# A depthwise convolution as small Toeplitz matrices over permuted tokens, in a hybrid attention and convolution layer

## The chip, the cores and the metric

The kernel runs on all 8 cores of one Trainium2 chip, one sequence of the batch on each core, without communication. The metric is the device time of the slowest core, in microseconds (us). A second, slower state exists: in some executions the cores of one die show a lower TensorE clock (instead of 0.99) and the time is longer.

## The reference, cut to what matters

One decoder layer on x of 2048 tokens by 1024 features for each core:

```python
h = rmsnorm(x, g_mix_norm)
proj = h @ w_in + b_in                       # q | k | v | glu_in (2 x 512) | gates (2 x 1024)
y_attn = sliding_window_attention(q, k, v, sinks) @ w_attn_proj     # window 128, 8 heads of 64
a, b = split(glu_in);  z = a * sigmoid(b)    # GLU, 512 channels
z = causal_depthwise_conv(z, conv_w) + conv_b                       # 31 taps, one filter per channel
y_conv = silu(layernorm(z, ln_g, ln_b)) @ w_conv_proj + b_conv_proj
x = x + (gate0 * y_attn + gate1 * y_conv) @ w_out
x = x + (silu(gate) * up) @ w_ffn_down       # gate, up = rmsnorm(x) @ w_ffn_in, 2816 wide
return rmsnorm(x, g_final)
```

## The kernel before

Features lie on the partitions, tokens along the free dimension. Four parts follow one another: the **start** (first norms and projections), a **loop** over 16 attention blocks with the GLU and half of the convolution woven in, the **merge** (gates, the two output projections and the other half of the convolution), and the feed-forward part.

The convolution, 16 units (4 token groups by 4 channel tiles). SBUF-to-SBUF transfers lay four shifted copies of z under one another, so that a 128x32 weight block holds 4 taps of 32 channels on its diagonals. Four such blocks stand side by side in the array:

```python
def conv_unit(tg, c):
    for m in range(8):                       # 8 shifts x 4 taps = 32 taps
        for cg in range(4):                  # 4 x 32 channels, side by side
            mm(ps[bank][32*cg:32*(cg+1), :], wS[:, 4*c+cg, m, :],
               zs[half][:, c % 2, cg, 4*m:4*m+512], m == 0, m == 7, ..., tile_position=(0, 32*cg))
    act(y, ps[bank], AF.Identity, scale=0.5, bias=conv_b[...])     # ScalarE evicts ...
    act(ysq[tg][c], ps[bank], AF.Square, ...)                      # ... and squares, both from PSUM
    op("pool", tensor_copy(out=ybf[tg][c], in_=y))
# fill_zs(tg, half): 16 SBUF-to-SBUF transfers of 67.5 KB from zT
```

The start, in the order in which it is issued:

```python
for j, g in enumerate((0, 0, 0, 2, 4, 4)):
    load_qkv(j, r=["x.0.%d" % g])            # r: what the load waits for
load_x(1, xi[:, 1], r=["wqkv2"])             # second token group
...
p1_qk(0, (0, 1, 2)); p1_qk(0, (3, 4)); p1_v(0)      # projections of group 0
load_glu(0, r=["wqkv5"])                     # GLU weights, after x1
scores(0)
run(sqs)                                     # squares of x1; stats() below sums them on PE
glu_b(0, 0); glu_a(0, 0)
stats(); scores(1); run(norms[:4]); pv(0)
```

The softmax here doesn't subtract the row's maximum and nothing guards it: scores larger than these inputs give would overflow.

Of the kernel before, what the change touches and what calls it, by code (L numbers as in the profile page):

```python
# [14 lines left out]
D = 1024  # L15
T = 2048
# [181 lines left out]
def build_program():  # L198
# [10 lines left out]
    w_glu_d = din("w_glu", [4, 128, 2, 8, 128])  # L209
# [4 lines left out]
    NV = 210  # L214
    vec_d = din("vecs", [128, NV])
    wdiag_d = din("wdiag", [128, 16, 8, 32])
# [7 lines left out]
    def region(nbytes):  # L224
# [6 lines left out]
    X_OFF = region(66560)  # L231
# [3 lines left out]
    R_OFF = region(20480)  # L235
    VEC_OFF = region(NV * 4)
    HB_OFF = region(30 * 4)
    HLN_OFF = region(8 * 4)
# [8 lines left out]
    conv_b = vec[:, 30:34]  # L247
    ln_g = vec[:, 34:38]
    ln_b = vec[:, 38:42]
    bcp = vec[:, 42:50]  # L250
    g_mix = vec[:, 50:58]
    g_ffn = vec[:, 58:66]
    g_fin = vec[:, 66:74]
    sinks = vec[:, 74:82]
    bv_bc = vec[:, 82:210]
    hb = A.f32(HB_OFF, 30)
    hln = A.f32(HLN_OFF, 8)
# [5 lines left out]
    XB = X_OFF + 1024  # L263
# [5 lines left out]
    convT = A.bf16(CT_OFF, 4 * T).rearrange("p (c t) -> p c t", c=4)  # L269
    WS_OFF = R_OFF + 12288  # L270
    wS = A.bf16(WS_OFF, 16 * 8 * 32).rearrange("p (g m c) -> p g m c", g=16, m=8)
    ZSW = 544
    zs = [A.bf16(X_OFF + 8704 * i, 2 * 4 * ZSW).rearrange("p (h g t) -> p h g t", h=2, g=4)
          for i in range(2)]
    ysqoff = [[XB + 16384 + 1024 * c for c in range(4)]] * 4
    ysq = [[A.bf16(o, 512) for o in row] for row in ysqoff]

    hT = A.bf16(H_OFF, 8 * T).rearrange("p (c t) -> p c t", c=8)
    qT = A.bf16(M_OFF, 4 * T).rearrange("p (c t) -> p c t", c=4)
    kT = A.bf16(M_OFF + 16384, T)  # L280
    v_aug = A.bf16(M_OFF + 20480, 16 * 2 * 65).rearrange("p (n g d) -> p n g d", n=16, g=2)
    ZPAD = 32
    zT = A.bf16(M_OFF + 24640, 4 * (T + ZPAD)).rearrange("p (c t) -> p c t", c=4)
# [3 lines left out]
    NMIX = 4  # L287
    MIX_OFF = [R_OFF, R_OFF + 6144, W_OFF, W_OFF + 6144]
    w_mix_sb = [A.bf16(o, 3072).rearrange("p (s k m) -> p s k m", s=3, k=8) for o in MIX_OFF]
# [10 lines left out]
    class Tmp:  # L300
# [3 lines left out]
        def take(self, nbytes):  # L304
# [14 lines left out]
    yoff = [[CT_OFF + 4096 * c + 2048 for c in range(4)], [Y_OFF + 2048 * c for c in range(4)],  # L319
            [M_OFF + 16384 + 2048 * c for c in range(4)], [Y_OFF + 2048 * c for c in range(4)]]  # L320
    y32 = [[A.f32(o, 512) for o in row] for row in yoff]
    YB_OFF = t2.take(4 * 1024)
    ybfoff = [[CT_OFF + 4096 * c + 1024 for c in range(4)]] + [[YB_OFF + 1024 * c for c in range(4)]] * 3
    ybf = [[A.bf16(o, 512) for o in row] for row in ybfoff]
    ST_OFF = t2.take(2 * 2048)
    stA = A.f32(ST_OFF, 512)
    stB = A.f32(ST_OFF + 2048, 512)
    TB_OFF = t2.take(4096)
    tbl = A.f32(TB_OFF, 1024).rearrange("p (b t) -> p b t", b=2)
# [4 lines left out]
    iota_i = A.i32(PT_OFF, 128)  # L334

# [21 lines left out]
    NB2 = norm_bufs(PT_OFF, PT_OFF + 12288, PT_OFF + 8192, 4)  # L357
    w_out_sb = A.bf16(Y_OFF, 8 * 1024).rearrange("p (k n) -> p k n", k=8)
    nb = NB1

    ebuf = [A.f32(PT_OFF + 8192 * b, 2048).rearrange("p (k t) -> p k t", k=4) for b in range(2)]
# [64 lines left out]
    def load_x(tg, dst, r=()):  # L426
        for c in range(4):
            dma("sp", dst[:, 2 * c:2 * c + 2, :], x_d[tg, c], r=r,
                w=["x.%d.%d" % (tg, k) for k in (2 * c, 2 * c + 1)])
# [3 lines left out]
    M.claim("iota", PT_OFF, 512)  # L433
    claim_norm(NB1)
    for j in range(6):
        M.claim("wqkv%d" % j, R_OFF + 2048 * j, 2048)
    for c in range(4):
        M.claim("wglu%d" % c, W_OFF + 4096 * c, 4096)
# [4 lines left out]
    def load_glu(c, r=()):  # L443
        dma("pool", w_glu_sb[:, c], w_glu_d[c], r=r, w=["wglu%d" % c])
# [10 lines left out]
    op("pool", lambda e: e.memset(zT[:, :, 0:ZPAD], 0.0), w=["z_pad"])  # L455
    for j, g in enumerate((0, 0, 0, 2, 4, 4)):
        load_qkv(j, r=["x.0.%d" % g])
    load_x(1, xi[:, 1], r=["wqkv2"])
# [6 lines left out]
    M.claim("z_pad", M_OFF + 24640, 16640)  # L465
# [4 lines left out]
    def warm1():  # L470
        mm(ps[6][:, 0:256], ones[:, 0, :], ones.rearrange("p w m -> p (w m)"), True, True,
           r=["ones0", "ones1"], w=[P(6)])

# [4 lines left out]
    def sq_mm(stat, tg, src, c, first, last, eng="act"):  # L478
# [9 lines left out]
        def pe():  # L488
            for h in range(2):
                mm(ps[stat][:, :], ones[:, 0, :], n.sq[:, b, h, :], first and h == 0, last and h == 1,  # L490
                   r=["ones0", "sq%d" % b], w=[P(stat)])
# [34 lines left out]
    rot = Rot(list(range(7)))  # L526
    st_rot = Rot([7])
# [17 lines left out]
    def p1_tasks(tg):  # L545
        src = xi[:, tg % 2]
        stat = st_rot()
        pes = []

        def stats():  # L550
            for f in pes:
                f()
                if tg == 0:
                    warm(6)
            if tg == 0:
                warm(10)
            rstd(stat, tg)
# [6 lines left out]
    def qk_evac(tg, j, bank):  # L564
        dst, dn = (qT[:, j, tsl(tg)], "qT.%d" % tg) if j < 4 else (kT[:, tsl(tg)], "kT.%d" % tg)
        act(dst, ps[bank][:, :], AF.Identity, r=[P(bank), "vec"], w=[dn], bias=b_fm[:, j:j + 1])
# [10 lines left out]
    def p1_v(tg):  # L577
        bank = rot()
        for j in range(4):
            tt = 4 * tg + j  # L580
            for k in range(8):
                mm(ps[bank][:, j * 128:(j + 1) * 128], hT[:, k, tt * 128:(tt + 1) * 128],
                   w_qkv_sb[:, 5, k, :], k == 0, k == 7,
                   r=["wqkv5", "hT.%d.%d" % (tg, k)], w=[P(bank)])
# [671 lines left out]
```

## Time and profile before

| | before |
|---|---|
| median of 15 runs over all rounds | 902.55 us (the ten fast ones: 900.19 to 903.55, median 901.09) |
| spans of the 8 cores in the profiled run | 895.7 to 900.3 us, median 898.4 |
| TensorE busy | 868.3 us, 96% |
| convolution matmuls | 30.9 us |
| TensorE idle from 100 us to the end of the merge | about 1.5 us |

The main lines are shown in the prediction. Four more are needed later. First a window of the loop (length; then busy time and count of PE, PE's weight loads, VectorE, ScalarE and POOL; granted clock, DMA share, GB/s), then VectorE's timeline (start, length, what), the kind of transfer that fed the convolution (count, KB each, median us from issue to landing), and the longest piece of the chain that ended last.

```profile
100.00:150.00 50.00, 48.85 (x451) 24.60 (x453) 23.70 (x57) 30.83 (x51) 16.93 (x17) 1.00 0.39 83
...
27.79 3.30 DVE L397 TENSOR_TENSOR arena<-arena 128x1024 bf16<-128x1024 f32 x2
...
arena<-arena SPq DMA_DIRECT2D x128, 67.5 KB, 2.1
...
437.46 388.02 PE ps L391 x1797
```

In the loop PE is idle for about 1 us in 50. At 27.8 us VectorE squares its half of x1 (ScalarE squares the other half), early and undisturbed. The convolution's input comes in many small transfers that land in a median of 2.1 us. From 437 us on PE runs for 388 us in one piece: what is not won before that point is not won at all.

### The profile page before, as it was taken

The numbers are of one execution on the slowest core, as the hardware profiler recorded it, in microseconds if no ns is written. First come the engines' busy times: TensorE is split into PE (matmuls) and PEld (weight loads), VectorE is DVE, ScalarE is ACT, GpSimd is POOL, SyncE is SP. The second block draws the span as 40 slices with busy tenths as digits, with TensorE's granted clock in tenths as the row PEclk, the third lists the DMA queues.
The fourth block names the chain that finished last, engine by engine and source line by source line (L and its number), as shares of the span: only waits on it lengthen the run. The fifth ranks groups of instructions, "written<-read, shape, count | busy, mean of one in ns | idle before, by whom it ended". The sixth has DMA issues, their size and how long they took to land.

```text
span 900.3 us, 14199 instructions; the slowest of 8 cores (895.7 to 900.3 us)
## 1 busy us (share of the span) xinstructions
PE 868.3 (96%) x4782; PEld 401.3 (45%) x4782; DVE 392.6 (44%) x636; ACT 323.5 (36%) x469; POOL 135.0 (15%) x155
## 2 busy tenths in 40 slices
PE   7788999999999999999999999999999999999994
PEld 4343445444444444444444444444444444444443
DVE  2345453665573343468421353212451216435447
ACT  3557756766663433343311100111001110024453
POOL 2133223221320000131000000000000000012222
PEclk9899999999999999999999999999999999999998
DMA  9753315363229541500521330212501215002115
GB/s 204 197 142 48 84 42 116 78 129 92 96 94 153 105 67 28 187 0 1 94 48 24 60 58 1 48 25 45 83 1 24 41 30 83 0 1 94 47 48 187
DMA packets 27925, 65.44 MB, mean 73 GB/s; under 512 B 3536, under 2 KB 13904, under 8 KB 26960
## 3 DMA queue, kind: packets, MB, share of 16 engines
q0 software_dynamic: 9840, 30.41, 20.7%
q1 hardware_dynamic: 17328, 33.50, 12.0%
q8 instruction: 41, 0.67, 0.3%
q10 hardware_dynamic: 688, 0.63, 0.2%
q14 instruction: 28, 0.23, 0.1%
HBM read 77.70 MB, written 8.39 MB: 96 GB/s over the span
## 4 chain that ended last, share of the span: by engine, by line
PE 88%; DMA 3%; DVE 3%; issue 2%; ACT 2%; POOL 1%; DVEq 0%; SPq 0%; ACTq 0%; POOLq 0%
PE ps L391 88%; ACT arena L394 2%; DVE arena L407 2%; DMA arena<-w_qkv 1%; DMA arena<-w_glu 1%; DVE arena L397 1%; DMA arena<-x 1%; ACT L394 0%; PE ps L703 0%; POOL arena L397 0%; POOL arena L403 0%; DVEq L1181 0%; DVE arena L707 0%; DVE arena L694 0%; SPq L384 0%
## 5 line engine op out<-in xcount | busy, mean ns | idle before, releaser
L391 PE MATMUL ps<-arena 128*128 128x512 bf16 (+5 forms) x4718 | 866.7, 363 | 22.7 <-ACT arena L394 9.3
L391 PEld LDWEIGHTS ps<-arena 128*128 128x128 bf16 (+2 forms) x4718 | 397.1, 98 | 485.9 <-issue 62.3
L397 DVE TENSOR_TENSOR arena<-arena,ps 128x512 f32<-128x512 f32 (+1 forms) x216 | 147.6, 686 | 291.4 <-PE ps L391 276.5
L394 ACT ACTIVATE arena<-ps 128x512 f32<-128x512 f32 (+1 forms) x150 | 87.9, 596 | 342.3 <-PE ps L391 336.3
L407 DVE SCALAR_TENSOR_TENSOR arena<-arena 128x512 bf16<-128x512 f32 (+2 forms) x157 | 119.3, 794 | 119.5 <-ACT arena L394 112.1
L394 ACT ACTIVATE arena<-ps,arena 128x512 f32<-128x512 f32 (+2 forms) x193 | 127.2, 683 | 122.7 <-PE ps L391 121.7
L394 ACT ACTIVATE arena<-arena 128x512 f32<-128x512 f32 (+6 forms) x99 | 78.7, 815 | 82.9 <-DVE arena L407 40.8
L397 POOL TENSOR_TENSOR arena<-arena 128x512 bf16<-128x512 f32 (+2 forms) x35 | 42.7, 1226 | 195.3 <-ACT arena L394 182.6
L384 POOL DMA_DIRECT2D arena<-w_ffn_in x22 | 11.7, 534 | 347.2 <-PE ps L391 347.2
L397 DVE TENSOR_TENSOR arena<-arena 128x512 f32<-128x512 f32 (+2 forms) x72 | 51.6, 747 | 8.5 <-ACT arena L394 3.3
L394 ACT ACT_TABLE_LOAD x27 | 34.6, 1283 | 21.8 <-PE ps L391 11.1
L397 DVE TENSOR_TENSOR arena<-ps,arena 128x256 bf16<-128x256 f32 (+3 forms) x72 | 22.6, 333 | 30.0 <-PE ps L391 26.2
L407 DVE SCALAR_TENSOR_TENSOR arena<-arena,ps 128x512 f32<-128x512 f32 x32 | 21.9, 685 | 17.9 <-ACT arena L394 16.4
L407 DVE SCALAR_TENSOR_TENSOR arena<-ps,arena 128x512 f32<-128x512 f32 x32 | 21.7, 685 | 17.2 <-PE ps L391 17.2
L667 POOL TENSOR_SCALAR_AFFINE_SELECT arena<-arena 128x1024 bf16<-128x1024 bf16 x16 | 17.8, 1114 | 71.6 <-ACT arena L394 71.6
L403 POOL TENSOR_SCALAR arena<-arena 128x512 f32<-128x512 f32 x16 | 16.2, 1016 | 56.9 <-ACT arena L394 55.8
L672 POOL TENSOR_SCALAR_AFFINE_SELECT arena<-arena 128x1024 bf16<-128x1024 bf16 x15 | 17.4, 1162 | 1.4 <-issue 0.4
L731 POOL CAST arena<-arena 128x512 bf16<-128x512 f32 x16 | 12.2, 770 | 34.2 <-ACT arena L394 25.6
L707 DVE COPY arena<-ps 128x512 bf16<-128x512 bf16 x16 | 6.7, 419 | 15.3 <-PE ps L703 15.3
L384 POOL DMA_DIRECT2D arena<-w_mix x8 | 4.4, 548 | 25.4 <-PE ps L391 21.4
L694 DVE RECIPROCAL arena<-arena 128x4 f32<-128x4 f32 x32 | 5.7, 178 | 3.3
L703 PE MATMUL ps<-arena 128*128 128x128 bf16 x64 | 6.2, 219 | 0.7 <-ACT arena L394 0.7
(18 smaller groups left out, 21.3 us busy)
## 6 DMA issues: line engine op xcount, KB each, us to landing
arena<-x SPq DMA_DIRECT2D x32, 512.0 KB, 6.7
arena<-w_ffn_in POOLq DMA_DIRECT2D x22, 512.0 KB, 5.3
arena<-arena SPq DMA_DIRECT2D x128, 67.5 KB, 2.1
arena<-w_mix POOLq DMA_DIRECT2D x8, 768.0 KB, 12.7
out<-arena SPq DMA_DIRECT2D x6, 1024.0 KB, 3.9
arena<-w_ffn_down POOLq DMA_DIRECT2D x2, 1536.0 KB, 14.9
arena<-w_ffn_down POOLq DMA_DIRECT2D x2, 1280.0 KB, 13.8
arena<-w_glu POOLq DMA_DIRECT2D x4, 512.0 KB, 8.1
```

Source lines behind the costliest of these rows:

```text
L384: return S.add(eng, lambda e: e.dma_start(out=out, in_=in_, **kw), r=r, w=w, dma=True)
L391: return op("pe", lambda e: e.matmul(out=out, lhsT=lhsT, rhs=rhs, start=start, stop=stop, **kw), r, w)
L394: return op("act", lambda e: e.activation(out=out, in_=in_, func=func, **kw), r, w)
L397: return op(eng, lambda e: e.tensor_tensor(out=out, in0=in0, in1=in1, op=alu), r, w)
L403: return op(eng, lambda e: e.tensor_scalar(out=out, in0=in0, scalar1=s1, scalar2=s2, op0=op0, op1=op1), r, w)
L407: return op(eng, lambda e: e.scalar_tensor_tensor(out=out, in0=in0, scalar=scalar, in1=in1, op0=op0, op1=op1), r, w)
L667: op("pool", lambda e, pw=pw: e.affine_select(out=pw, in_=pw, pattern=[[0, 8], [1, 128]], compare_op=ALU.is_ge, fill=0.0, base=0, channel_ ...
L672: op("pool", lambda e, pw=pw: e.affine_select(out=pw, in_=pw, pattern=[[0, 8], [-1, 128]], compare_op=ALU.is_gt, fill=0.0, base=0, channel ...
L694: op("dve", lambda e, dg=dg: e.reciprocal(out=dg, in_=dg), r=[dres], w=[dres])
L703: op("pe", lambda e, c=c: e.transpose(out=ps_bf[bank][:, c * 128:(c + 1) * 128], in_=attn_tm[:, b, c * 128:(c + 1) * 128], identity=ident) ...
L707: op("dve", lambda e: e.tensor_copy(out=attnT[:, :, n * 128:(n + 1) * 128], in_=ps_bf[bank][:, 0:512].rearrange("p (c j) -> p c j", c=4)), ...
L731: op("pool", lambda e: e.tensor_copy(out=ybf[tg][c], in_=y), r=[yr], w=["ybf.%d" % c])
```

## The change

The intent: less TensorE work in the convolution. The tokens of each sequence are permuted so that the position modulo 4 can be moved onto the partitions. A weight block then is a small Toeplitz matrix, in: 4 shifts x 8 channels x 4 phases, out: 8 channels x 4 phases, and 3 shifts instead of 8 cover the 31 taps. Its core:

```diff
-        for m in range(8):
-            for cg in range(4):
-                mm(ps[bank][32 * cg:32 * (cg + 1), :], wS[:, 4 * c + cg, m, :],
-                   zs[half][:, c % 2, cg, 4 * m:4 * m + 512], m == 0, m == 7, ...
+        for bl in range(4):
+            for si, sh in enumerate((5, 1, 0)):
+                for j in range(4):
+                    mm(ps[bank][32 * j:32 * (j + 1), o:o + 256], wT[:, c, 4 * bl + j, si, :],
+                       zs[zb][:, 4 * bl + j, sh:sh + 256], si == 0, si == 2, ...
-        act(y, ps[bank], AF.Identity, ...); act(ysq, ps[bank], AF.Square, ...)
+        for i, bank in enumerate(banks):
+            tt_("dve", y32[:, c, 2 * i:2 * i + 2, :], ps[bank], conv_b[...], ALU.add, ...)
+        act(ysq[:, c], y32[:, c], AF.Square, r=[yr], w=["ysq.%d" % c])
```

The permutation has followers: z goes to DRAM in 256-byte pieces and comes back in 512-byte ones (32 fills of about 260 KB), the LayerNorm runs over two halves instead of four groups and ends in one Silu, 32 rearranging copies bring its output back to channels on partitions, keys and values are written with a stride, and V is projected transposed. Around it the schedule was rewritten:

```diff
-    for j, g in enumerate((0, 0, 0, 2, 4, 4)):
-        load_qkv(j, r=["x.0.%d" % g])
-    load_x(1, xi[:, 1], r=["wqkv2"])
+    for j in range(6):
+        load_qkv(j, r=["x.0.%d" % (2 * j)] if j < 4 else ["wqkv%d" % (j - 4)])
+    load_glu(0, 1, r=["wqkv2"])
+    load_glu(0, 0, r=["wqkv3"])
+    load_x(1, xi[:, 1], r=[["wqkv4"], ["wqkv5"], ["wglu0.1"], ["wglu0.0"]])
...
-    scores(0); run(sqs); glu_b(0, 0); glu_a(0, 0); stats(); ...
+    glu_b(0, 0); glu_a(0, 0); run(sqs); scores(0); p1_v(0); warm_fill(4); stats(); ...
```

(cut: the merge, in which the gated convolution branch now follows three tiles behind the attention branch; buffers; host-side packing of weights and x.)

## The prediction

> **What bounds the kernel now.** I read the list of cores first (spans 895.7 to 900.3 us, clocks 0.988 to 0.994, both dies 898.4 and 898.5: undisturbed), then the page's busy times, the slices, a table of windows, the groups by form, and the chain that ended last.
>
> ```profile
> PE 868.3 (96%) x4782; PEld 401.3 (45%) x4782; DVE 392.6 (44%) x636; ACT 323.5 (36%) x469; POOL 135.0 (15%) x155
> PE   7788999999999999999999999999999999999994
> PEclk9899999999999999999999999999999999999998
> ```
>
> TensorE is busy for 96% of the span, every other engine for less than half. The slices show where it is not full: the first four and the last.
>
> ```profile
> 0.00:50.00 50.00, 37.57 (x213) 18.94 (x214) 17.59 (x28) 23.51 (x31) 11.20 (x23) 0.93 0.81 189
> 50.00:100.00 50.00, 45.18 (x316) 21.21 (x316) 23.30 (x60) 34.92 (x52) 13.66 (x13) 0.93 0.40 94
> 200.00:250.00 50.00, 49.95 (x372) 21.87 (x367) 30.33 (x44) 29.59 (x46) 12.58 (x14) 1.00 0.32 92
> 300.00:350.00 50.00, 50.00 (x233) 22.70 (x232) 20.22 (x30) 19.51 (x29) 2.64 (x5) 1.00 0.37 64
> ```
>
> After the window, its length comes PE, PE's weight loads, VectorE, ScalarE, POOL, then granted clock, DMA share and GB/s. From 300 on nothing but 512-column matmuls run: 233 in 50 us, **0.215 us each**, without a gap. From 100 to 829 us PE has about 1.5 us of idle time in all, so there only less PE work can save time. Before 100 us PE idles 17 us (12.4 and 4.8) and runs at a granted clock of 0.93, so there waits count.
>
> ```profile
> L391 PE MATMUL ps<-arena 128*32 128x512 bf16 x512 | 30.9, 380 | 0.0
> L391 PE MATMUL ps<-arena 128*128 128x256 bf16 x160 | 21.0, 289 | 5.3 <-ACT arena L394 3.0 <-DVE arena L450 1.7 <-DVE arena L397 0.7
> L391 PE MATMUL ps<-arena 128*128 128x65 bf16 x248 | 10.7, 193 | 1.1 <-ACT arena L394 1.0
> L391 PE MATMUL ps<-arena 128*128 128x128 bf16 x128 | 7.8, 219 | 0.1
> ```
>
> These are the parts of PE's time that the change touches. Busy time over count is the spacing: the convolution's 512 matmuls with 32-column weights take 30.9 us, **60 ns each**, against 215 ns for a full 512-column one, so four of them share the array. The value projection is the row of 128 matmuls: 61 ns each. The attention's 65-column matmuls (43 ns each) show how fast a weight load and a short matmul can follow one another.
>
> ```profile
> 1.98 7.76 DMA arena<-x
> ...
> 10.78 11.48 DMA arena<-w_qkv
> 22.79 9.13 DMA arena<-w_glu
> ...
> 43.02 3.74 DVE arena L407 x3
> 48.44 0.75 DVE arena L407
> 49.32 4.45 PE ps L391 x12
> ```
>
> This is the start of the chain (start, length, what). The GLU weights arrive only at 31.9 us, and PE has waited 4.7 us for them; then the normalisation of the second token group holds the next projection until 49.3 us.
>
> **What the Trainium skill says.** "TensorEngine Tiling (Array Packing)", Key Properties: different tiles load weights and multiply in parallel, and a change of tiling mode drains the array. The trace agrees on the first: 60 against 215 ns. "TensorE: Matmul & The Clock Gate", Part 1: start-to-start of matmuls does not fall below about 25 ns however short they are. This trace's shortest spacing is 43 ns, with a weight load in each pair. "DMA: Bandwidth & Descriptors", Specifications: transfers below 512 B are read-modify-write; Anatomy of one DMA: about 2 us are fixed. The trace's 67.5 KB fills land in a median of 2.1 us, which fits the second; nothing in it tests the first, which the new 256-byte writes will meet.
>
> **The change part by part.**
>
> 1. *The convolution's arithmetic.* Before, a weight block held 4 taps of 32 channels on its diagonal, and 8 shifts of 512 positions were needed: 16 units of 32 matmuls. After, tokens are permuted so that the position modulo 4 becomes part of the partition index; a weight block is a small Toeplitz matrix (8 channels by 4 phases out, 4 shifts by 8 channels by 4 phases in), and 3 shifts cover the 31 taps. There are 2 halves x 4 channel tiles x 48 matmuls = 384, each of 256 columns. In streamed columns per array quarter that is 384 x 256 / 4 = 24.6 thousand against 512 x 512 / 4 = 65.5 thousand. If the present overhead per group of four (4 x 60 - 215 = 25 ns) stays, a group takes 107 + 25 = 132 ns, 33 ns per matmul; if the pair of load and short matmul binds, 43 ns. I take 38: 384 x 38 = 14.6 us instead of 30.9. **PE work -16.3 us** (-18.2 to -14.4), all of it where PE has no idle time, so all of it on the path.
>
> 2. *The value projection.* Its 128 matmuls (7.8 us) become 32 of 512 columns (32 x 0.215 = 6.9 us) and 16 transposes (the 64 present transposes take 6.2 us on the page, 0.1 each: 1.5 us). **+0.6 us**. Its bias moves into the ScalarE evacuation.
>
> 3. *LayerNorm sums.* 32 matmuls of 512 columns become 64 of 256: about the same, 6.9 us. Nothing.
>
> 4. *Order of the loads at the start.* The first GLU weights are split and come before the second group of x. By 31.9 us the core had loaded, in source bytes, x0 2.1, qkv 3.1, x1 2.1, GLU 1.05 MB and part of the next: about 9 MB in 30 us, 0.3 MB/us. Ahead of GLU 0 there will be x0 and qkv alone, 6.3 MB with itself: estimated at 23 to 25 us. PE then is the limit: it began the first projection at 16.4 us and, at the pace of the norm and then 0.215 us per matmul, ends its 48 at about 27. So the first GLU starts near 27 and not at 32.1, and the squares of x1, the 8 sum matmuls, rstd and norm, which followed it on the chain, all move up by as much, since x1 (8.4 MB in all) is there by about 30. **-5 us**. Four filling matmuls lie in PE's idle time there: 0.
>
> 5. *Stalls from 70 to 91 us.* PE lost about 5 us there to ScalarE and VectorE around the norm of the third group. The new order has the sums and the whole norm one step earlier, with about 10 us of PE work between them and the projection, and the sums no longer keep a PSUM bank to themselves. I count **-2 us**.
>
> 6. *ScalarE and VectorE.* The LayerNorm ends in one Silu instead of Tanh, a POOL scale-and-shift and a VectorE multiply; fewer instructions, and two passes instead of four, so fewer table loads (27 now, 1.28 us each). None of that is on the path from 100 to 829 us. Nothing.
>
> 7. *Transfers.* The 128 SBUF-to-SBUF fills (67.5 KB) become 16 writes to DRAM in pieces of 256 B, 32 fills of about 262 KB in pieces of 512 B, and 32 rearranging copies after the LayerNorm. In the first half each has about three loop steps (some 25 us) to land: hidden. In the merge the third and fourth fill wait for a buffer that the first and second tile leave, some 17 us before they are needed. The queue rows give 1728 us of engine time for 17328 packets, 100 ns a packet of 1.9 KB; if a 512-byte one takes 65 ns (my guess), a fill of 2048 pieces on 16 engines takes 8 us, plus about 5 us for a mix-weight load beside it, plus 2. It fits, barely. Against this, and for ScalarE where two passes of exponentials, Ln, Exp and Silu meet at the end of the loop, I add **+2 us**.
>
> Sum: -16.3 + 0.6 - 5 - 2 + 2 = -20.7 us. The two fast runs before were 902.85 and 900.85, and the profiled one 902.05; from 902.2 that gives **881.5 us**, a ratio of 0.977.
>
> **The rivals.** *A: the transfers become the bound in the merge.* PE would wait for the third or fourth fill, or for the rearranged output before the gated projection of the second half. For: the margin in step 7, a DRAM round trip, the 256-byte writes. Against: DMA share is 0.32 from 200 to 250 us, and the gated convolution branch is delayed by three tiles, which gives some 15 us. It would cost 3 to 10 us: 885 to 892. *B: small matmuls do not overlap.* With 32-column weights and only 256 columns, loads and issue may bind at 60 ns each as now: 384 x 60 = 23 us, a gain of 8 only: 890. For: spacing did not reach the ideal 54 before. Against: the 43 ns pairs. *C: the start is bound by HBM anyway.* DMA share is 0.81 in the first 50 us; if the reordering only moves the wait from the GLU weights to x1, step 4 gives 0 to 2: 885. *D: VectorE binds in the merge*, with 2.3 us of it per 5.2 us of PE plus LayerNorm passes of 1024 elements: about 23 us of work in 25 us of PE for five tiles. A short backlog, at most 3 us, since the buffers are four deep.
>
> **Range and chances.** The convolution alone gives 14 to 18 us, just below the 2% line, which lies at 18 us (884.8 us from 902.85). The start and stalls add 2 to 9, the new waits take 0 to 8. I take 871 to 892 for 8 in 10. Only if the start yields or the waits stay away does it cross 2%: faster 0.66, within 2% 0.31, slower 0.03.
>
> **What would show it.** Step 1: a group of 128x32 weights with 256 columns, 384 of them, with 13 to 16.5 us of busy time. Step 4: the GLU wait in the chain ends before 28 us, and the second group's projection starts near 44 us and not 49.3. Step 5: PE busy over 47 us from 50 to 100. Step 7: PE idle under 2 us between 100 us and the end of the merge, no DMA row among PE's waits. From the end of the merge on, both traces should be equal in length; if they are not, or if PE waits for a fill or for a rearranging copy, the prediction is wrong there.

## More of the kernel before

A helper gives every operation its waits, so one line of the program stands for all matmuls (L391 before, L393 after), one for all ScalarE activations (L394, then L396), one for VectorE's two-tensor operations (L397, then L399).

## The result, and the profile after

| | before | after |
|---|---|---|
| median | 902.55 us (15 runs) | 893.69 us (12 runs, 891.27 to 1047.24) |
| median of the fast runs | 901.09 us (10) | 893.43 us (9, 891.27 to 896.83) |
| ratio, 95% interval | | 0.9912, 0.9895 to 0.9929: the same within 2% |
| spans of the 8 cores | 895.7 to 900.3, median 898.4 | 883.9 to 891.5, median 888.0 |
| TensorE busy | 868.3 us | 851.7 us |

Ratios are the mean time of one kernel's fast runs over that of the other's of the same rounds, so not quite the ratio of the medians. Executions in which one die ran at a lower clock are left out of the means. The prediction, 881.5 us with a range of 871 to 892, was too low. Of the expected 20.7 us some 8 came in the slowest core (0.9912), and 10.4 in the median of the cores. The rest of the argument goes by the medians of the cores; why the slowest core gained 2 us less is not shown.

The page of the kernel after, its busy times and slices, then windows of the table of windows:

```profile
PE 851.7 (96%) x4610; PEld 399.4 (45%) x4610; DVE 386.0 (43%) x619; ACT 316.2 (35%) x459; POOL 127.5 (14%) x141
...
PE   7879989899999999999999999999999999999994
```

```profile
0.00:50.00 50.00, 38.23 (x196) 18.99 (x197) 16.63 (x29) 25.04 (x32) 14.02 (x25) 0.96 0.83 186
50.00:100.00 50.00, 46.39 (x311) 21.24 (x310) 26.30 (x64) 38.21 (x54) 16.25 (x13) 0.97 0.52 116
100.00:150.00 50.00, 45.10 (x440) 22.70 (x439) 27.33 (x64) 30.31 (x46) 18.45 (x17) 1.00 0.90 133
200.00:250.00 50.00, 47.96 (x323) 23.90 (x316) 22.78 (x33) 20.27 (x29) 4.08 (x5) 0.97 0.47 79
```

PE works 16.6 us less, but the span falls by less: from 100 to 150 us PE idles 4.9 us where it idled 1.2, from 200 to 250 us 2.0 where it idled 0.05, and the DMA share from 100 to 150 us went from 0.39 to 0.90. In the first 50 us next to nothing changed.

The groups by form that answer to those of before (the transposes of V are L597):

```profile
L393 PE MATMUL ps<-arena 128*32 128x256 bf16 x384 | 12.5, 280 | 2.0 <-DMA arena<-z_scratch 2.0
...
L597 PE MATMUL ps<-arena 128*128 128x128 bf16 x16 | 1.6, 219 | 0.4 <-ACT arena L396 0.4
```

The start of the chain, and its longest piece:

```profile
2.45 11.73 DMA arena<-x
...
15.47 18.14 PE ps L393 x84
35.99 1.23 DVE arena L399
...
42.97 4.09 DVE arena L409 x3
48.73 0.75 DVE arena L409
49.62 4.80 PE ps L393 x14
...
428.68 388.03 PE ps L393 x1797
```

PE now runs from 15.5 to 33.6 us without waiting for GLU weights, and yet the second projection starts at 49.62 us, where it started at 49.32. From the end of the merge on the two kernels are equal (388.03 against 388.02), as foreseen.

To find where time was gained and lost I took one mark for each part: the start of the transposes that follow attention block 0, 8 and 15, as a median over the eight cores.

| interval | before | after | change |
|---|---|---|---|
| start to block 0 | 54.9 | 53.5 | -1.4 |
| block 0 to 8 | 59.8 | 58.9 | -0.9 |
| block 8 to 15 (half of the convolution) | 58.3 | 61.0 | **+2.7** |
| block 15 to the end | 725.4 | 714.6 | -10.8 |
| sum | 898.4 | 888.0 | -10.4 |

The runs further down tell how well a mark repeats where a run left a stretch as it is in the kernel after: start to block 0 came to 53.5 to 54.8 us in eight, block 8 to 15 to 60.6 to 61.2 in five, block 15 to the end to 712.0 to 715.5 in eight. So the +2.7 is clear, while the -1.4 at the start is the best of eight (the worst is -0.1), and the 714.6 after block 15 can move by 1 to 3 us.

What PE's own work would have given is worked out from the durations in the traces. A unit of the convolution took 1.84 us before, a tile takes 1.43 us after, and LayerNorm sums take 1.7 us per group before and 3.5 per half after. In the loop 7 units (-12.9) and one set of sums (-1.7) leave; four tiles (+5.7), one set of sums (+3.5) and half a GLU tile that is now ahead of the last mark (+1.7) come: 54.6 us, where 61.0 were measured. **6.4 us were lost in the loop.** After block 15, 9 units (-16.6), three sets of sums (-5.2) and that half GLU tile (-1.7) leave, four tiles (+5.7) and one set of sums (+3.5) come: -14.3, where -10.8 were measured. **3.5 us were lost in the merge**, 0.9 to 4.4 with the spread just named. PE's waits there say the same without a subtraction: on the eight cores of the profiled run 0 to 3.3 us for fills of z, about 2 in the median, and 1.3 to 1.5 more before the last gated tile.

The waits are on PE's timeline (start, length, what, and in brackets the idle time before it and what ended it), and in two cases on ScalarE's:

```profile
124.59 13.79 PE L393 MATMUL ps<-arena 128*128 128x512 bf16 x104 [1.09 <-ACT arena L396]
149.05 9.19 PE L393 MATMUL ps<-arena 128*128 128x512 bf16 x100 [0.89 <-ACT arena L396]
171.37 0.38 PE L732 MATMUL ps<-arena 128*128 128x128 bf16 x4 [1.78 <-ACT arena L396]
176.22 0.38 PE L732 MATMUL ps<-arena 128*128 128x128 bf16 x4 [0.52 <-DVE arena L399]
219.55 55.08 PE L393 MATMUL ps<-arena 128*32 128x256 bf16 x304 [2.04 <-DMA arena<-z_scratch]
```

```profile
122.90 1.06 ACT L396 ACTIVATE arena<-arena 128x1024 bf16<-128x1024 f32 x1 [4.30 <-DVE arena L399]
123.86 2.44 ACT L396 ACTIVATE arena<-ps 128x512 bf16<-128x512 f32 x4
147.36 1.06 ACT L396 ACTIVATE arena<-arena 128x1024 bf16<-128x1024 f32 x1 [2.93 <-DVE arena L399]
```

The first and third ScalarE lines are the Square of a convolution tile. It waits 4.30 and 2.93 us for VectorE's eviction, and the four exponentials of the next block (second line), for which PE waits in turn, stand behind it. These two gaps make 2.0 us. All gaps of PE over 0.1 us, whatever ended them, are eleven from 100 to 180 us on the profiled core and add up to 7.8 us; before they were three, 1.15 us. The difference of 6.6 agrees with the 6.4.

The page's transfers of z show what took the place of the 67.5 KB fills (16 of them; the other 16 have 256.0 KB and a median of 9.4 us):

```profile
arena<-z_scratch SPq DMA_DIRECT2D x16, 261.0 KB, 10.8
```

### The profile page after: what moved, and what is told of

Same layout as the page of the kernel before. It is cut to its first block, busy times and chain, and to the rows that moved or that the text cites. A ratio compares the mean times of both kernels' runs of the same rounds, so it can differ in the third digit from the quotient of the medians.

```text
span 891.5 us, 13544 instructions; the slowest of 8 cores (883.9 to 891.5 us)
## 1 busy us (share of the span) xinstructions
PE 851.7 (96%) x4610; PEld 399.4 (45%) x4610; DVE 386.0 (43%) x619; ACT 316.2 (35%) x459; POOL 127.5 (14%) x141
## 3 DMA queue, kind: packets, MB, share of 16 engines
q1 hardware_dynamic: 35888, 36.79, 16.6%
## 4 chain that ended last, share of the span: by engine, by line
PE 83%; DVE 4%; ACT 4%; issue 3%; DMA 3%; SPq 1%; DVEq 0%; POOL 0%; ACTq 0%; POOLq 0%
PE ps L393 83%; ACT arena L396 4%; DVE arena L399 2%; DVE arena L409 2%; DMA arena<-z_scratch 1%; DMA arena<-x 1%; SPq L386 1%; ACT L396 0%; POOL arena L399 0%; PE ps L732 0%; DMA arena<-arena 0%; DVEq L1238 0%; DVE arena L736 0%; DVE arena L723 0%; DVEq L152 0%
## 5 line engine op out<-in xcount | busy, mean ns | idle before, releaser
L393 PE MATMUL ps<-arena 128*128 128x512 bf16 (+3 forms) x4530 | 848.6, 357 | 27.6 <-ACT arena L396 13.6
L393 PEld LDWEIGHTS ps<-arena 128*128 128x128 bf16 (+1 forms) x4530 | 394.6, 98 | 474.5 <-issue 56.2
L409 DVE SCALAR_TENSOR_TENSOR arena<-arena 128x512 bf16<-128x512 f32 (+2 forms) x141 | 110.6, 820 | 113.0 <-ACT arena L396 113.0
L396 ACT ACTIVATE arena<-ps,arena 128x512 f32<-128x512 f32 (+1 forms) x165 | 113.7, 716 | 116.1 <-PE ps L393 68.8
L396 ACT ACTIVATE arena<-arena 128x256 bf16<-128x256 f32 (+7 forms) x121 | 91.2, 762 | 104.7 <-DVE arena L399 54.3
L399 DVE TENSOR_TENSOR arena<-arena 128x512 bf16<-128x512 f32 (+3 forms) x54 | 46.7, 878 | 4.1 <-DVE arena L409 0.8
L399 DVE TENSOR_TENSOR arena<-ps,arena 128x4 f32<-128x4 f32 (+3 forms) x82 | 28.9, 369 | 16.5 <-PE ps L393 12.2
L696 POOL TENSOR_SCALAR_AFFINE_SELECT arena<-arena 128x1024 bf16<-128x1024 bf16 x16 | 20.8, 1299 | 61.2 <-ACT arena L396 61.2
L701 POOL TENSOR_SCALAR_AFFINE_SELECT arena<-arena 128x1024 bf16<-128x1024 bf16 x15 | 20.9, 1395 | 0.0
L761 POOL CAST arena<-arena 128x1024 bf16<-128x1024 f32 x8 | 8.3, 1038 | 52.1 <-DVE arena L399 52.1
L732 PEld LDWEIGHTS ps<-arena 128*128 128x128 bf16 x64 | 4.3, 97 | 7.4 <-issue 5.8
## 6 DMA issues: line engine op xcount, KB each, us to landing
arena<-z_scratch SPq DMA_DIRECT2D x16, 261.0 KB, 10.8
arena<-z_scratch SPq DMA_DIRECT2D x16, 256.0 KB, 9.4
```

Source lines behind the costliest of these rows:

```text
L393: return op("pe", lambda e: e.matmul(out=out, lhsT=lhsT, rhs=rhs, start=start, stop=stop, **kw), r, w)
L396: return op("act", lambda e: e.activation(out=out, in_=in_, func=func, **kw), r, w)
L399: return op(eng, lambda e: e.tensor_tensor(out=out, in0=in0, in1=in1, op=alu), r, w)
L409: return op(eng, lambda e: e.scalar_tensor_tensor(out=out, in0=in0, scalar=scalar, in1=in1, op0=op0, op1=op1), r, w)
L696: op("pool", lambda e, pw=pw: e.affine_select(out=pw, in_=pw, pattern=[[0, 8], [1, 4], [4, 32]], compare_op=ALU.is_ge, fill=0.0, base=0, c ...
L701: op("pool", lambda e, pw=pw: e.affine_select(out=pw, in_=pw, pattern=[[0, 8], [-1, 4], [-4, 32]], compare_op=ALU.is_gt, fill=0.0, base=0, ...
```

## The experiments

All kernels give the reference's result unless it is said otherwise. One time or a median is given; block marks are medians over the eight cores of one profiled execution. The rounds ran on four chips or more, where the kernel before took 900.9 to 903.4 us (medians of fast runs or single runs), so times of different rounds are compared only roughly; ratios are to the kernel before of the same rounds.

### The start: e1, e2, e10

My theory: the reordered loads only moved the wait, from the GLU weights to x1 (rival C of the prediction). The transfers say so: GLU 0 landed at 29.2 us (31.9 before), but the last quarter of x1 at 34.2 (28.9 before), since it is issued behind the QKV and GLU weights. The rival: the order of the work alone is at fault. VectorE's timeline after:

```profile
35.38 0.69 DVE L409 SCALAR_TENSOR_TENSOR arena<-arena 128x512 bf16<-128x512 f32 x1 [11.85 <-ACT arena L396]
35.99 2.35 DVE L399 TENSOR_TENSOR arena<-arena 128x1024 bf16<-128x1024 f32 x2
```

VectorE's half of x1's squares (second line, at 35.99; at 27.79 before) stands in its queue behind the product of the GLU (first line).

**e1, squares first.** Only the order of work changes:

```diff
+    run(sqs)
     glu_b(0, 0)
     glu_a(0, 0)
-    run(sqs)
```

> The changed kernel with one move in the start: the squares of the second token group are emitted before the first GLU tile and not after it, loads as they are. In the changed kernel the last chunk of x1 lands at 34.2 us, VectorE squares only from 36.0 (behind the GLU product) and the second projection starts at 49.6. Theory A (the landing of x1 is what holds the start): the second projection moves by less than 1 us, since the last square can start at 34.2 at the earliest. Theory B (the queue order on VectorE and ScalarE holds it): sums about 2 us earlier, second projection near 47.5.

Measured, single look: 894.15 us; block 0 at 52.1 us, against 53.5 to 54.8 in the looks without the edit: -1.4 to -2.7. On the profiled core the second projection starts at 47.48 us instead of 49.62, which is what the text gave to Theory B: the order of the work alone is worth some 2 us. (The slowest core ended at 892.5 us, the median of the cores at 885.1.)

**e2, x1 first.** x1 is loaded ahead of the GLU weights as before, and its sums run before the GLU (left out: the waits of the loads that follow):

```diff
-    load_glu(0, 1, r=["wqkv2"])
-    load_glu(0, 0, r=["wqkv3"])
-    load_x(1, xi[:, 1], r=[["wqkv4"], ["wqkv5"], ["wglu0.1"], ["wglu0.0"]])
+    load_x(1, xi[:, 1], r=[["wqkv2"]] * 4)
+    load_glu(0, 1, r=["wqkv5"])
+    load_glu(0, 0)
...
-    glu_b(0, 0); glu_a(0, 0); run(sqs); scores(0); p1_v(0); warm_fill(4); stats(); scores(1); run(norms[:4]); pv(0)
+    run(sqs); scores(0); p1_v(0); warm_fill(4); stats(); glu_b(0, 0); run(norms[:4]); glu_a(0, 0); scores(1); pv(0)
```

> The changed kernel with the old order of loads (qkv, then x1, then the GLU weights) and with squares, sums and rstd of the second group ahead of the first GLU tile on PE. Theory A (the wait moved from the GLU weights to x1, and the norm of the second group is the chain): x1 lands near 29 us, the norm starts near 36 and not 42.3, the second projection starts at 42 to 44 and not 49.6, and the whole is 5 to 7 us shorter than the changed kernel, about 887. Rival (the start is bound by the bytes from HBM whatever the order): the second projection stays within 2 us of 49.6 and the time within 2 us of 893.7.

Measured: **887.73 us**, the median of three fast runs (887.17 to 892.08; with the slow fourth it is 889.91), ratio 0.9854 (0.9819 to 0.989); block 0 at 50.3 us: -3.2. In the four later runs with this start it came at 50.3 to 50.7. PE's timeline of e2 shows one unbroken piece over the place where the second projection had to wait:

```profile
32.64 16.62 PE L393 MATMUL ps<-arena 128*128 128x512 bf16 x91
```

**e10, keys and values without the stride** (a wrong result, relative error 0.106):

```diff
-            dst = d.rearrange("p (n h) -> p h n", h=4)
+            dst = d.rearrange("p (h n) -> p h n", h=4)
```

> Wrong result on purpose: keys and values are evicted in the permuted token order, without the stride of four elements in the writes. The strided evictions take about 1.3 us and the plain ones 0.69 in the changed kernel. Theory G (they hold up ScalarE ahead of the second group's squares and the GLU tanh at the start): the transposes of blocks 0 and 2 come 1 to 1.5 us earlier. Rival: they lie beside the wait for x1, under 0.4 us.

Measured, single look: 894.33 us; block 0 at 51.2 us (-2.3), block 8 at 110.2 (-2.2). In the changed kernel ScalarE's strided evictions of K and V take 1.39 and 1.41 us each, without the stride 0.69; in the start the next work of ScalarE stands behind them. Whether it lasts to the end is not shown: the median of the cores is 886.2 us, against 888.0 here and 886.6 to 889.3 in the nine fast runs of the kernel after, and the slowest core, at 892.6, shows no gain.

So rival C held in that the wait moved from the GLU weights to x1. What it says of HBM, that the start is bound by the bytes whatever their order, e2 refutes. Two things count: when x1 lands, and where its squares stand in the queues.

### The loop: e3, e9, e4, e8, e6

Theory: PE waits because VectorE and ScalarE pass the convolution tile and the LayerNorm along a chain that stands in front of the attention's exponentials and evictions. Rival: PE is not the bound there any more and its work no longer counts.

**e3, square and cast later.** The Square on ScalarE and the cast on POOL of each tile in the loop are put behind the next step's exponentials:

```diff
-        act(ysq[:, c], y32[:, c], AF.Square, ...)
-        op("pool", lambda e: e.tensor_copy(out=ybf[:, c], in_=y32[:, c]), ...)
+        def squares(): ...            # both of them
+        if h == 1: squares()
+        else: pend.append(squares)    # run one step later, after glu_b
```

> The changed kernel with the squares (ScalarE) and casts (POOL) of a first-half convolution tile emitted after the next step's exponentials and GLU tanh. Theory C (in the loop ScalarE stands at the square, which waits for VectorE to evict the tile, and the exponentials queue behind it, so PE waits for banks): the gaps of 1.1 us before the GLU matmuls at steps 9 and 11 go to under 0.3 us, the loop from 115 to 176 us is 2 to 3 us shorter. Rival (PE waits because PE itself became faster and the engines behind it are full): the gaps move elsewhere and the loop is shorter by under 1 us.

Measured: 893.51 us (the four fast ones of five: 893.34), ratio 0.9905 (0.9887 to 0.9923): **no gain**. Both gaps are gone, but the last tile's cast now stands behind two of POOL's select operations, and the LayerNorm sums wait for it:

```profile
155.73 2.34 PE L393 MATMUL ps<-arena 128*128 128x256 bf16 x20 [1.86 <-POOL arena L764]
```

**e9, the square only.** As e3, with the cast left in its place:

```diff
+        def squares():
+            act(ysq[:, c], y32[:, c], AF.Square, ...)
         op("pool", lambda e: e.tensor_copy(out=ybf[:, c], in_=y32[:, c]), ...)
```

> The mended form of the third experiment: only ScalarE's square is emitted after the next step's exponentials, the POOL cast stays where it was (in the third experiment the last cast, queued behind two selects, made the LayerNorm sums wait 1.9 us). Theory C: the two gaps of 1.1 and 0.9 us go and nothing takes their place; from the transpose of block 8 to that of block 15 it is 59 us instead of 61.0. Rival (the gaps only move): 60.5 or more.

Measured, single look: 893.58 us; block 8 to 15 in 60.0 us, against 61.0. One microsecond of the 6.4 is this. PE, earlier by the gap at 124.6, meets the next limit, the fill of the following tile:

```profile
126.44 1.50 PE L393 MATMUL ps<-arena 128*32 128x256 bf16 x48 [1.64 <-DMA arena<-z_scratch]
```

**e4, without the mean pass.** The LayerNorm's subtraction of the mean is left out in the first half. That is wrong mathematics; its effect on the final result was too small to fail the comparison.

```diff
-        12: [lambda: a2(0), a1, lambda: a2(1)], 13: [lambda: a2(3), lambda: a3(1)],
+        12: [a1], 13: [lambda: a3(1)],
-    end = {12: [lambda: a2(2), lambda: a3(0)]}
+    end = {12: [lambda: a3(0)]}
```

> Wrong result on purpose: the subtraction of the mean is left out in the first half's LayerNorm, 4 VectorE passes of 1024 elements, 1.17 us each. Theory D (at the end of the loop the passes stand before the attention's own VectorE work, and the transposes of blocks 14 and 15 wait for it): the gaps of 1.8 and 0.5 us before the transposes at 171.4 and 176.2 us go to under 0.3 us, the loop ends about 2 us earlier. Rival (ScalarE with exponentials, Ln, Exp, Silu and two table loads is what holds): the gaps stay, the loop ends within 0.7 us of 176.6.

Measured, single look: 894.79 us; block 12 to 15 in 17.1 us, against 18.2. The gap before the transposes of block 14 fell from 1.78 to 1.39 us, the one of block 15 vanished. VectorE's passes are one part of the cause. For the wait that stays the trace names ScalarE (Ln, Exp, Silu and two table loads of 1.28 us stand there); e4 does not test that.

**e8, the LayerNorm later.** All passes of the first half come after the attention's evictions, two Silu steps in the merge:

```diff
-    12: [a2(0), a1, a2(1)], 13: [a2(3), a3(1)], 14: [a3(2), a3(3)]; end 12: [a2(2), a3(0)]; a4(i - 13) for i > 12
+    12: [a2(0)], 13: [a1, a2(1), a2(2)], 14: [a2(3), a3(0), a4(0)], 15: [a3(1), a3(2), a4(1)]; merge 0: [a3(3), a4(2), a4(3), ...]
```

> Result stays right: the first half's LayerNorm is spread over one step more at the end of the loop, with Ln, Exp and Silu and the VectorE passes behind the attention's own evictions, and the last two Silu groups at the start of the merge. Theory D, second form (the transposes of blocks 14 and 15 wait both for the VectorE passes and for the table loads on ScalarE ahead of them in the same queues): the gaps of 1.8 and 0.5 us go to under 0.3, the stretch from the transpose of block 12 to that of block 15 is 16 us instead of 18.2. Rival: the wait moves to the merge's first gated tile, and the end is not earlier by more than 0.7 us.

Measured, single look: **902.53 us**, 9 us slower. Block 12 to 15 fell to 16.2 us, 2.0 better than 18.2, so the gap in the loop has the cause that I gave it. But the rearranging copies now come late, and the merge's first gated tile waits for them:

```profile
194.93 20.29 PE L393 MATMUL ps<-arena 128*128 128x512 bf16 x165 [8.09 <-DMA arena<-arena]
```

**e6, the convolution of the loop done twice** (same result, 5.7 us more of PE work):

```diff
-            for si, sh in enumerate((5, 1, 0)):
+            for si, sh in (list(enumerate((5, 1, 0))) * (2 if h == 0 else 1)):
```

> The first half's four convolution tiles are multiplied twice (the second time overwrites the first, the result stays right): 192 more matmuls, 4 x 1.43 = 5.7 us of PE work in the loop. Theory F (in the loop PE has lost its full occupancy, so PE work there is partly free): the loop from the transpose of block 8 to that of block 15 grows by 2 to 4 us, and part of the saving of the new convolution was never to be had there. Rival (PE still bounds the loop and its gaps are fixed costs): it grows by 5.3 to 5.9 us.

Measured, single look: 900.06 us; block 8 to 15 +4.8, the end +5.7. The 4.8 lie between what the text gave to Theory F (2 to 4) and to its rival (5.3 to 5.9): at most about 1 us of the added work went into time in which PE would have waited. So the rival named at the head of this part falls. PE work in the loop counts nearly in full; the gaps are added to it and hide little.

### The merge: e5, e7

Theory: the third and fourth fill of z are late (rival A). Rival: VectorE holds the merge (rival D).

**e5, without the late fills** (a wrong result, relative error 0.229):

```diff
-            if k < 2:
-                fill_zs(1, k + 2)
```

> Wrong result on purpose: in the merge the third and fourth convolution tile read the buffers that the first two filled, and their own eight fills from DRAM are left out. Theory E (the fills that must wait for a free buffer land late): PE's wait for the scratch tensor before the fourth tile goes, the merge from the last transpose to the end is 1 to 3 us shorter in the median core and the cores lie closer together. Rival (the merge loses its time elsewhere, to the late LayerNorm copies): under 0.7 us.

Measured, single look: 889.18 us; block 15 to the end -2.8 us (-2.1 as the median of the differences core by core), the slowest core -3.9. Runs that keep the fills reach 712.0 us there, as against 711.8 here, so the mark alone would not show it. PE's waits do: the 0 to 3.3 us for fills are gone on every core. PE's timeline has one piece over the merge, where the kernel after stopped at 219.55:

```profile
176.23 94.43 PE L393 MATMUL ps<-arena 128*128 128x512 bf16 x616
```

**e7, the convolution of the merge done twice**: e6's edit with `h == 1`.

> The same in the second half, whose tiles lie in the merge: 5.7 us more PE work. If PE bounds the merge the time from the last transpose to the end grows by 5.3 to 5.9 us less what PE now waits for the late fills (about 1.5 us in the median core): 4 to 5.9. If the merge is bound by transfers or by VectorE it grows by under 3.

Measured, single look: 903.06 us; block 15 to the end +3.2 for 5.7 us of work (+4.6 core by core), between the "4 to 5.9" and the "under 3" of the text, so by itself it decides little. PE's waits for fills are gone on seven of the eight cores: part of the added work took their place. The wait for the last copies grew to 1.8 to 3.5 us. So rival A explains most of the 3.5 us, by PE's waits about 2 in the median core, and no wait of PE for VectorE shows in the merge (rival D). About the rest is the last gated tile, which waits for the rearranging copies of the second half or, on other cores, for ScalarE: 1.29 us at 275.92 in the kernel after.

### Putting it together: e11, e12, e13, e14

**e11, combined**: e2 and e9; the transposes of blocks 14 and 15 later; the second LayerNorm's passes in a denser order; the mix weights of merge tile 4 loaded before the merge and those of tile 5 one convolution tile later, so as not to lie beside the late fills.

```diff
+ e2's loads and order, e9's squares
-        return [], [], [(attn_t, i)] + ([(pv, i + 1)] if i < 15 else [])
+        (transposes of 13, then 14; that of 15 in the merge)
-        if oi == 4: load_mix(4)      # and tile 5 after convolution tile 1
+        load_mix(4)                  # ahead of the merge; tile 5 after convolution tile 2
```

> Result right. All that the experiments point to: x1 ahead of the GLU weights with its squares and sums first; squares later; the transposes of blocks 14 and 15 one and two steps later; the fifth mix-weight load ahead of the merge and the sixth after the third convolution tile, out of the way of the fills; the second half's LayerNorm one step shorter. If the named waits are the cause and each is worth what it measured (3.2 to 4.6 at the start, 2.0, 2.3, 1 to 2.5 and 1.3 us), the time is 10 us below the changed kernel, about 883 to 885. If waits only move, 888 or more.

Measured: 891.15 us, ratio 0.9873 (0.9852 to 0.9894), not better than e2. The named gaps are gone, but a new one of 4.5 to 6.5 us, by core, stands before the first gated tile, for the rearranging copies.

**e12**: as e11, the transposes back in their place, the mix weights of tile 4 two steps earlier than in the changed kernel.

```diff
-        if oi == 4: load_mix(4)
+        if oi == 2: load_mix(4)
```

> Combines what helped one at a time: x1 loaded ahead of the GLU weights and its sums ahead of the GLU in the loop's start (gained 3.2 us at block 0 and 4 in the end), the Square of a loop's conv tile behind the next step's exponentials (gained 1 us in the loop alone), the LayerNorm passes of the second half in a denser order so that the last rearranging copy comes earlier (1.3 us wait before), and in the merge the mix weights of tile 4 loaded two steps earlier and those of tile 5 one convolution tile later, so that they are not beside the last two fills (a wait of 2.0 us, 2.8 in the run without late fills). The transposes at the end of the loop stay where they are, because moving them let TensorE reach the first gated tile 5.6 us before its copies. If the gains add: block 0 at 50.4 us, blocks 8 to 15 in 59.5 to 60 us, no wait for a fill over 0.5 us between 180 and 225 us, and 885 to 888 us at the end, 0.981 to 0.984 of before. Rival: the waits are one chain of transfers (fills, copies and weight loads share the queues and engines), so that what is gained at the start is waited for at the next transfer: then it comes out as x1 first alone did, 889 to 891 us, with a wait for a fill or a copy of 2 us or more in the loop or the merge.

Measured: 889.67 us, ratio 0.9855 (0.9836 to 0.9873; the profiled execution, 896.03 us, is the slowest of the five): the rival of that text held. The wait for fills is gone, and a wait for copies is there, 2.1 to 4.8 us on the eight cores.

Two explanations of the late copies stayed. Theory G: the weight load shares the transfer engines with them. Theory H: they stand in SP's queue behind writes of z that wait for the GLU.

**e13, the load of tile 4 back**: `if oi == 4: load_mix(4)` again, the rest as e12.

> As e12, but the mix weights of tile 4 are loaded where the changed kernel loads them, after the first copies. Theory G (shared engines): in e12 that 1.5 MB load was issued at 171.8 us and landed at 182.0, amid the rearranging copies, which took 10 us from issue to landing and 3.3 to 5 us in e2; without it they land about 1.5 us earlier, the wait at the first gated tile falls from 3.8 us on the profiled cores' median to 2 or less, and the end comes at 886 to 888 us. The price: the load lies beside the last fills again, but that of tile 5 does not, so a wait of under 1 us there. Theory H (order of issue): the copies come after three writes of the convolution's input in one queue, the last of which waits until 172 us for the GLU; then the load changes nothing, the wait stays at 3 to 5 us and the time at 889 to 890.

**e14, all 16 copies issued by POOL**, the rest as e13:

```diff
-                dma("pool" if h == 0 and c < 2 else "sp", convT[...], cb[q:128:4], ...)
+                dma("pool" if h == 0 else "sp", convT[...], cb[q:128:4], ...)
```

> As e13, but all 16 rearranging copies of the first half are issued by POOL, so that those of the third and fourth tile no longer stand behind the writes of the convolution's input in the queue of SP. Theory H (order of issue): they are issued as soon as their Silu is done, some 3 us earlier than at 173 to 182 us, and the wait at the first gated tile falls to under 1 us: 1 to 2 us better than e13. Theory G (shared engines): what they wait for is the transfer engines, full of the 1 MB fill issued at 159 us; issued earlier they land as late as in e13, within 1 us, and the time is that of e13.

Measured: e13 **884.91 us** (five runs, 884.42 to 886.34), ratio 0.9824 (0.9811 to 0.9837): it beats both kernels. The interval overlaps that of e2, so its lead over e2 is not shown by the slowest core; the medians of the cores, over the fast runs, are 880.9 and 884.2. e14: 892.19 us, the median of five fast runs (894.60 with the two slow ones), ratio 0.9902 (0.9883 to 0.9921). PE's timeline at the first gated tile, of e12, then e13, then e14:

```profile
185.35 9.83 PE L393 MATMUL ps<-arena 128*128 128x512 bf16 x79 [3.78 <-DMA arena<-arena]
```

```profile
168.04 16.92 PE L393 MATMUL ps<-arena 128*128 128x512 bf16 x118 [0.22 <-ACT arena L396]
```

```profile
184.98 7.28 PE L393 MATMUL ps<-arena 128*128 128x512 bf16 x64 [5.58 <-DMA arena<-arena]
```

In e13 PE passes the first gated tile within one piece, without the wait. Over the cores the wait for copies is 2.1 to 4.8 us in e12, 0 to 0.7 in e13 and 1.3 to 5.9 in e14. The single transfers (core 0; us) show why:

| | the last copies issued | they landed | what else was under way |
|---|---|---|---|
| e12 | 8, at 173.1 to 181.8 | 183.1 to 185.1 | mix weights of tile 4, issued 171.8, landed 182.0 |
| e13 | 8, at 171.3 to 177.2 | 175.8 to 179.4 | the fill of z comes after them, at 177.9 |
| e14 | the last 4, at 174.5 to 176.1 | 179.9 to 184.7 | a fill of z (four transfers, 1 MB), issued 173.1 to 175.1, landed 177.5 to 184.6 |

The transfers by kind from 170 to 186 us, first e13, then e14 (count, KB, median us from issue to landing):

```profile
arena<-arena SPq DMA_DIRECT2D x8, 64.0 KB, 2.2
```

```profile
arena<-arena POOLq DMA_DIRECT2D x8, 64.0 KB, 4.4
```

Neither theory had e14 right. The engines are shared, as G said: whatever bulk transfer is issued ahead of the copies delays them, the weights in e12, the fill in e14. The order of issue matters too, but the other way round than H had it: SP's queue did not hold the copies up, it held the **next fill** back until they were issued. With the copies moved to POOL, SP issued that 1 MB fill first. The other cores of e14 bear it out: where the fill was issued ahead of the last four copies (cores 0, 2, 3, 5 and 7), PE waited 4.6 to 5.9 us, and where it came later (cores 1, 4 and 6), 1.3 to 2.4. The Trainium skill states the first half ("DMA: Bandwidth & Descriptors", Issuing engines are not separate DMA queues): transfers of all issuing engines run on the same 16 engines and interleave. The runs agree, with 7.3 us between the fast runs of e13 and e14, or 5.1 by the medians of the cores.

## Why the prediction was wrong

The convolution's arithmetic was right. What failed is step 4 (the path: it followed the wrong load), step 6 ("nothing", where 6.4 us were lost in the loop; 3.0 of them are shown to come from the order in ScalarE's and VectorE's queues) and the size in step 7 (15 us for a fill, where it took 17.3 to 19.3).

1. **Step 1 (-16.3 us) was right, and somewhat better: -17.9** (16 units of 1.84 us became 8 tiles of 1.43). A matmul takes 30 ns. That is the case "overhead stays" and not better: from the same spacing the matmuls before take 57.5 ns, not 60, and step 1's sum with it gives 30.5 instead of 33. Rival B (60 ns) is refuted. The group's busy time of 12.5 us lies below the 13 to 16.5 that I named as proof.
2. **Steps 2 and 3 were right**: the value projection came to +0.3 instead of +0.6, the sums to nothing.
3. **Step 4 (-5 us) failed; rival C took its place.** The GLU wait did vanish, as the step has it, and the two halves of GLU 0 landed at 25.1 and 29.2 us where 23 to 25 was estimated. But "x1 is there by about 30" was wrong: 34.2. The step followed the load that PE waited for and not the one that the next link, the squares of x1, would wait for, and it took the squares to move with the GLU when they had been put behind it. Result: -1.4 at best instead of -5. e2 gave 3.2 us more by putting x1 and its sums first; of these some 2 are the order of the work (e1). The strided evictions of K and V (0.7 us more each), which no step mentions, are a further part (e10: 2.3 us at block 0).
4. **Step 5 (-2 us) was smaller**: -0.9 from block 0 to 8. PE busy from 50 to 100 us came to 46.4 us, not over 47.
5. **Step 6 ("nothing") and step 7 (+2 us) are the larger part of the error: the new waits took about 9.9 us**, 6.4 in the loop and 3.5 in the merge. Step 6 counted busy time on ScalarE and VectorE and found room. What counts is the order in the queue: the Square waits up to 4.3 us with the exponentials behind it (e9: 1.0 us), and the LayerNorm passes stand in front of the attention's evictions (e8: 2.0 us). The other 3.4 us of the loop are read from PE's gaps alone; no run tests their causes. The Trainium skill's "PSUM — Partial Sum Buffer", Engine vs sequencer instructions, says that the queues of ScalarE, VectorE and POOL are strictly first in, first out; the trace agrees, with the exponentials at 123.86 right behind a Square that had waited 4.30 us. In step 7 "it fits, barely" did not hold. The guess of 65 ns for a 512-byte piece was fair (51 to 57 on the profiled core), and the 256-byte writes, which the prediction left open, are no slower by the byte (22 ns each). A transfer lands after a median of 9.4 to 10.8 us, near my 8 + 2, and those of the fourth tile, beside a mix-weight load, 13 to 15 us after their issue, as in my 8 + 5 + 2. What the sum lacks is the issue itself: a tile's fill is four transfers, SP issued them one after the other at 200.4 to 206.3 us, and the last landed at 219.3. So the fill took 18.9 us (17.3 to 19.3 on the eight cores) where the sum has 15 and PE came for it after 17. PE waited about 2 us for fills in the median core, 3.3 at most, and 1.3 for the last copies: rival A at its lower end.

The terms as measured: -17.9 + 0.3 - 1.4 - 0.9 + 9.9 = -10.0 us, against -10.4 for the medians of the cores. (The 9.9 is itself a remainder, so this sum closes by construction; PE's gaps, 6.6 us more in the loop and 3.3 in the merge on the profiled core, are the independent check. And the forecast's starting point of 902.2 is 0.3 above the mean of the three times that it names, which changes nothing.) With the start, the square, the fills and the weight loads mended, e13 is 6.7 us better by the same medians (881.3 against 888.0): 3.0 up to block 0, and 3.1 after block 15. In the loop, about 5 us of the 6.4 stay. Which of the smaller gaps there could be closed without a new wait, no run shows: e8 and e11 moved the largest ones and paid more in the merge.

## What to carry to other kernels

When a kernel is bound by one engine at 96%, taking work from it is worth that work only if nobody in the chain around it gets slower: ask of each new operation not how busy its engine is, but what stands behind it in its queue. When a load is moved forward, list what it overtakes, and compute when that now lands. And before small urgent transfers are given a queue of their own, look at which bulk transfer the old queue kept behind them.

## What the Trainium skill lacked or had wrong

- "TensorEngine Tiling (Array Packing)", Theoretical Speedup, gives "up to 4x" and no duration for four column tiles of 32; no page has a measured one. The traces have 57.5 ns per matmul at 512 columns and 30 ns at 256, so four in 230 and 120 ns, where a full 512-column matmul takes 215.
- "DMA: Bandwidth & Descriptors", Anatomy of one DMA, fits a duration by total bytes (about 2 us and bytes over 436e3 per us), for transfers issued from GpSimd. For these fills, issued from SP in pieces of 522 B, it is far too short: four of 261 KB issued from 182.6 to 184.6 us in e12 landed at 187.1 to 192.4. That is 9.9 us for 1.04 MB, or 7.3 from the landing of the last copy ahead of them at 185.1, where the fit gives 4.4. What part of this the pieces have (57 to 70 ns each) and what part other transfers, no run separates. No page has a time measured on trn2 for pieces of about 512 B.
- The same page, Issuing engines are not separate DMA queues: it is right that the engines are shared, but it names the saved issue time as the only effect of another issuing engine. In e14 the other effect, that a bulk transfer is no longer held back behind small ones, cost 7.3 us.
- "ScalarE: Activation LUTs", What ACT_TABLE_LOAD costs, has ACTIVATE at one element per cycle without regard to its output pattern; no page has a time for one that writes with a stride. Writing 512 bf16 elements with a stride of 4 took 1.39 us, without it 0.69 us (kernel after against e10).
